# A hybrid encoder block on one core: the opening of its projection, the order of its tokens and the shape of its last products rearranged

## The chip, the cores and the metric

One core of a Trainium2 chip runs the kernel. The metric is the device time of one execution in microseconds (us), median over runs. The engines are TensorE (PE; its weight loads are shown apart as PEld), VectorE (DVE), ScalarE (ACT), GpSimd (POOL) and SyncE (SP), which here only starts DMAs.

## The reference

One layer over 256 tokens of width 1024, all in float32:

```python
h = rmsnorm(x, norm_gain)
z = h @ w_in                       # 8192 columns: pool-in, pool-gate, q, k, v, attention gate, merge gates
a_in, a_gate, q, k, v, b_gp, g_logits = split(z)
y_a = (multiscale_pool(a_in, w_pool, pool_scale) * silu(a_gate)) @ w_proj_a
att = dilated_attention(q, k, v, rel_bias)     # 3 groups of 8 heads, (window, dilation) (128,1) (512,4) (2048,16)
y_b = (att * silu(b_gp)) @ w_proj_b
gates = sigmoid(g_logits + b_gate)
merged = gates[0] * y_a + gates[1] * y_b
return rmsnorm(x + merged @ w_out, final_gain)
```

## The kernel before

**Split products.** A float32 product is made of three passes: each operand is cut into a high part (a copy rounded to fp32r) and a low part (the operand minus its high part), and `mm3` (L253) multiplies high by high, high by low and low by high into one PSUM accumulator. The normalised tokens are `hh` and `hl`, 128 x 8 x 256 each, with the 1024 channels on partitions in eight blocks `kc`, and the 256 tokens sorted by their residue modulo 4.

**Weights.** SP streams all weights in the order of the list `order` (L82 to L90) through four buffers `wraw`: 31 tiles of `w_in` with 256 columns each (1 MB), then the pooling map, the two branch projections and `w_out`. `cut_half` (L116) makes half a tile's high part on ACT (L128) and its low part on DVE (L133), and starts the next load when a buffer is free. The cuts run two tiles ahead of the products.

**The opening (L170 to L250).** Its order on ACT, DVE, PE and POOL is written out by hand. PE first multiplies a zero tile (`keep_warm`, L177): 12 calls, two instructions each. The two blocks of 128 tokens come by DMA; their mean squares are taken on ACT and DVE, POOL makes the reciprocal root (L191), and DVE and ACT scale half the columns each (`XN`, L194 and L195). DVE copies the two halves (four `kc` rows each) of weight tile 0 to its high part (L197), and behind each copy POOL makes that half's low part (`cut_lo`, L163). PE turns `XN` over with 8 transposes a block (`turn`, L202), two `keep_warm` calls behind the first block and one behind the second. Per `kc`, ACT then writes `hh` (L228) and DVE `hl` (L229) out of PSUM, read with a step of four tokens so that they land by residue. PE takes tile 0 (`part0`, L207): per `kc` a pair of high by high products and a pair of high by low ones, two `kc` behind ACT and DVE; the pairs with the low weights follow for `kc` 0 to 3 behind step 5 and for 4 to 7 at the end, and then three small products for the bias lines (L245). Then `cut_next` makes both parts of tiles 1 and 2. The fills of the bias table (L486) are tied behind POOL's last low part.

**The middle.** Key, query, value, pooling, gate and attention stages follow, all as products with the 256 tokens; the rest of the order is the scheduler's.

**The end (L638 to L731).** `out_mm(kh, nh, tb)` (L674) multiplies token block `tb` with columns `nh` (512) and channels `kh` (half of them): 12 products of 512 columns, but for `nh` = `tb` = 1, which goes as two times 256. Behind the second half of the channels DVE adds the residual `XL` (L689), ACT squares with a sum (L691), DVE multiplies by the gain (L695), `finish` (L701) adds the sums on DVE and takes the root on POOL (L710), and `store` (L713) scales columns 0 to 639 on DVE and the rest on ACT and sends the block in two DMAs of 64 tokens, one by SP and one by ACT, with DRAM rows 4 apart. `XL` is loaded by POOL in four DMAs of 64 tokens (L661).

Of the kernel before, what the change touches and what calls it, by code (L numbers as in the profile page):

```python
# [11 lines left out]
F32 = mybir.dt.float32  # L12
# [17 lines left out]
LROW = 9  # L30
LAG_T, LAG_O = 2, 2
RATES = 0.5, 0.667
WARM = 12, 2, 1
CUT = 640
POOL_W = (2, 4, 8, 16)
PAD = 8
# [6 lines left out]
def encoder_block(ctx: ExitStack, tc: tile.TileContext, x, w_in, lines, w_pool, w_proj_a, w_proj_b,  # L43
# [126 lines left out]
    with tc.manual_schedule(engines={mybir.EngineType.Activation, mybir.EngineType.DVE, mybir.EngineType.PE,  # L170
                                    mybir.EngineType.Pool}):
        tiny = sb.tile([P, 1], F32, name="tiny")
        warm = sb.tile([P, P], F32, name="warm")
        nc.vector.memset(warm, 0.0)
        nc.scalar.activation(tiny, warm[:, 0:1], AF.Square)

        def keep_warm(times):  # L177
            for _ in range(times):
                nc.tensor.matmul(misc[:, P:2 * P], warm, warm, start=True, stop=True)

        keep_warm(WARM[0])
        halves = [slice(h * 512, (h + 1) * 512) for h in range(2)]
        for b in range(2):
            sq = [slot([P, 512], F32, "st", f"sq{b}{h}", 3) for h in range(2)]
            nc.scalar.activation(sq[0], X[:, b, halves[0]], AF.Square, scale=1.0 / 32.0, accum_out=ss[:, b, 0:1])
            xb = X[:, b, halves[1]]
            nc.vector.tensor_tensor_reduce(sq[1], xb, xb, scale=1.0 / D, scalar=EPS, op0=ALU.mult, op1=ALU.add,
                                           accum_out=ss[:, b, 1:2])
            t = slot([P, 1], F32, "rt", f"rt{b}", 2)
            nc.vector.tensor_tensor(t, ss[:, b, 0:1], ss[:, b, 1:2], op=ALU.add)  # L190
            nc.gpsimd.tensor_tensor(rs[:, b:b + 1], t, mhalf, op=ALU.pow)  # L191
        open_parts(0)
        for b in range(2):
            nc.vector.tensor_scalar(XN[:, b, halves[0]], X[:, b, halves[0]], rs[:, b:b + 1], None, op0=ALU.mult)  # L194
            nc.scalar.activation(XN[:, b, halves[1]], X[:, b, halves[1]], AF.Copy, scale=rs[:, b:b + 1])  # L195
        for k in (0, 4):
            nc.vector.tensor_copy(parts[0][0][:, k:k + 4, :], raws[0][0][:, k:k + 4, :])  # L197
            first_lo = cut_lo(0, k, k + 4, nc.gpsimd)
        tps = [bank([P, 2, S], "mm" if i < 3 else "T", f"tp{i}", 3 if i < 3 else 2) for i in range(4)]

        def turn(kc, b):
            nc.tensor.transpose(tps[kc % 4][:, kc // 4, b * P:(b + 1) * P], XN[:, b, kc * P:(kc + 1) * P], ident)  # L202

        acc = bank([P, 2, 512], "S", "k00", 1)
        acc0 = [acc[:, u, 0:S] for u in range(2)]

        def part0(kc, lo):  # L207
            hi_, lo_ = parts[0]
            for u in range(2):
                c = slice(u * P, (u + 1) * P)  # L210
                if not lo:
                    nc.tensor.matmul(acc0[u], hi_[:, kc, c], hh[:, kc, :], start=kc == 0, stop=False)
                else:
                    nc.tensor.matmul(acc0[u], lo_[:, kc, c], hh[:, kc, :], start=False, stop=kc == KC - 1)
            for u in range(0 if lo else 2):
                c = slice(u * P, (u + 1) * P)
                nc.tensor.matmul(acc0[u], hi_[:, kc, c], hl[:, kc, :], start=False, stop=False)

        for kc in range(KC):
            turn(kc, 0)  # L220
        keep_warm(WARM[1])
        for kc in range(KC):
            turn(kc // 2 + kc % 2 * 4, 1)
        keep_warm(WARM[2])
        for kc in range(KC):
            v = tps[kc % 4][:, kc // 4].rearrange("p (j r) -> p r j", r=4)
            gcol = prm[:, kc:kc + 1]
            nc.scalar.activation(hh[:, kc, :].rearrange("p (r j) -> p r j", r=4), v, AF.Copy, scale=gcol)  # L228
            nc.vector.scalar_tensor_tensor(hl[:, kc, :].rearrange("p (r j) -> p r j", r=4), v, gcol,  # L229
                                           hh[:, kc, :].bitcast(F32).rearrange("p (r j) -> p r j", r=4),  # L230
                                           op0=ALU.mult, op1=ALU.subtract)
            if kc >= 2:
                part0(kc - 2, False)
            if kc == 5:
                for k in range(4):
                    part0(k, True)
        part0(6, False)
        part0(7, False)
        for kc in range(4, 8):
            part0(kc, True)  # L240

        for t in range(3):
            w = 3 * NH
            o = 3 * P + t // 2 * w
            nc.tensor.matmul(misc[:, t * w:(t + 1) * w], oh[:, t * P:(t + 1) * P], oh[:, o:o + w],  # L245
                             start=True, stop=True)
        cut_next()
        nc.vector.tensor_copy(line.rearrange("p i r h -> p r i h"),
                              misc[:, 0:LROW * NH].rearrange("p (r i h) -> p r i h", i=2, h=4))
        cut_next()  # L250
# [404 lines left out]
        nc.vector.tensor_tensor(ML[:, cb, :], GA[:, cb, :], MH[:, cb, :].bitcast(F32), op=ALU.subtract)  # L655

    XL = slot([P, 2, D], F32, "v", "XL", 2)
    xr = x2.rearrange("(j r) d -> r j d", r=4)
    orr = o2.rearrange("(j r) d -> r j d", r=4)
    for r in range(4):  # L660
        nc.gpsimd.dma_start(XL[(r % 2) * 64:(r % 2) * 64 + 64, r // 2, :], xr[r])  # L661
    fg = slot([P, D], F32, "uu", "fg")
    nc.gpsimd.dma_start(fg, final_gain.rearrange("(o d) -> o d", o=1).to_broadcast([P, D]))

# [3 lines left out]
    accs = {}  # L668
    both = bank([P, 2, 512], "S", "both", 1)
    wo = {}  # L670
    so = sb.tile([P, 2, 3], F32, name="so")
    Y = slot([P, 2, D], F32, "q", "Y")

    def out_mm(kh, nh, tb):  # L674
        hi, lo = wo[kh, nh]
        c = slice(tb * P, (tb + 1) * P)
        cuts = 2 if (nh, tb) == (1, 1) else 1
        w = 512 // cuts
        for i in range(cuts):
            if kh == 0:  # L680
                accs[nh, tb, i] = both[:, tb, :] if nh == 0 else bank([P, w], "mm", f"out{nh}{tb}{i}", 3)
            acc = accs[nh, tb, i]
            for k in range(4):
                kc = kh * 4 + k
                mm3(acc, MH[:, kc, c], ML[:, kc, c], hi[:, k, i * w:(i + 1) * w], lo[:, k, i * w:(i + 1) * w],
                    kc == 0, kc == KC - 1)
            if kh == 1:
                cols = slice(nh * 512 + i * w, nh * 512 + (i + 1) * w)
                nc.vector.tensor_tensor(XL[:, tb, cols], acc, XL[:, tb, cols], op=ALU.add)  # L689
                j = slot([P, 512], F32, "st", f"j{tb}{nh}{i}", 3)  # L690
                nc.scalar.activation(j[:, :w], XL[:, tb, cols], AF.Square, scale=1.0 / 32.0,  # L691
                                     accum_out=so[:, tb, nh + i:nh + i + 1])
                if (nh, i) == (1, cuts - 1):
                    finish(tb, cuts)
                nc.vector.tensor_tensor(Y[:, tb, cols], XL[:, tb, cols], fg[:, cols], op=ALU.mult)  # L695
        if (kh, nh) == (1, 1):
            store(tb)

    scales = {}

    def finish(tb, cuts):  # L701
        t = slot([P, 1], F32, "nm", f"s2{tb}", 3)
        if cuts == 2:
            t0 = slot([P, 1], F32, "rl", f"s1{tb}", 3)
            nc.vector.tensor_tensor(t0, so[:, tb, 0:1], so[:, tb, 1:2], op=ALU.add)
            nc.vector.tensor_scalar(t, t0, so[:, tb, 2:3], EPS, op0=ALU.add, op1=ALU.add)
        else:
            nc.vector.tensor_scalar(t, so[:, tb, 0:1], so[:, tb, 1:2], EPS, op0=ALU.add, op1=ALU.add)
        r2 = slot([P, 1], F32, "l", f"r2{tb}", 3)
        nc.gpsimd.tensor_tensor(r2, t, mhalf, op=ALU.pow)  # L710
        scales[tb] = r2

    def store(tb):  # L713
        r2 = scales[tb]
        nc.vector.tensor_scalar(Y[:, tb, 0:CUT], Y[:, tb, 0:CUT], r2, None, op0=ALU.mult)
        nc.scalar.activation(Y[:, tb, CUT:], Y[:, tb, CUT:], AF.Copy, scale=r2)
        for rl in range(2):
            (nc.sync, nc.scalar)[rl].dma_start(orr[2 * tb + rl], Y[rl * 64:rl * 64 + 64, tb, :])

    wo[0, 0] = weights(n)  # L720
    for tb in range(2):
# [50 lines left out]
def _layout(x, norm_gain, w_in, b_gate, rel_bias, w_pool, pool_scale, w_proj_a, w_proj_b, w_out, final_gain):  # L772
# [11 lines left out]
    for k in range(3):  # L784
        for j, g in enumerate((0, k)):
# [4 lines left out]
    prm.append(np.broadcast_to(edges.reshape(1, -1), (P, edges.size)))  # L790
    prm.append(np.zeros((P, NPRM - sum(a.shape[1] for a in prm)), np.float32))
    w_out = np.concatenate([cols(w, 512) for w in np.split(np.asarray(w_out)[0], 2)])
    out = {"x": x, "w_in": cols(np.asarray(w_in)[0], 256), "lines": lines.reshape(99, -1),
           "w_pool": np.asarray(w_pool)[0].transpose(1, 0, 2), "w_proj_a": cols(np.asarray(w_proj_a)[0], 512),
           "w_proj_b": cols(np.asarray(w_proj_b)[0], 512), "w_out": w_out, "final_gain": final_gain,
# [24 lines left out]
```

## Time and profile before

| | us |
|---|---|
| median of three runs (lowest, highest) | 263.88 (263.72, 265.59) |
| the profiled execution: its own time | 264.12 |
| its span, first to last instruction | 262.30 |
| PE busy | 249.7 |
| DVE busy | 209.3 |
| ACT busy | 164.6 |
| POOL busy | 72.6 |

The span is what the trace covers; the profiled execution's own time holds 1.82 us around it. Times in the trace count from the span's start. Merged rows give a start, the time from the first start to the last end, and a count.

### The profile page before, as it was taken

The numbers are of one execution on the slowest core, as the hardware profiler recorded it, in microseconds if no ns is written. First come the engines' busy times: TensorE is split into PE (matmuls) and PEld (weight loads), VectorE is DVE, ScalarE is ACT, GpSimd is POOL, SyncE is SP. The second block draws the span as 40 slices with busy tenths as digits, with TensorE's granted clock in tenths as the row PEclk, the third lists the DMA queues.
The fourth block names the chain that finished last, engine by engine and source line by source line (L and its number), as shares of the span: only waits on it lengthen the run. The fifth ranks groups of instructions, "written<-read, shape, count | busy, mean of one in ns | idle before, by whom it ended". The sixth has DMA issues, their size and how long they took to land.

```text
span 262.3 us, 5321 instructions
## 1 busy us (share of the span) xinstructions
PE 249.7 (95%) x2088; PEld 245.0 (93%) x2088; DVE 209.3 (80%) x397; ACT 164.6 (63%) x283; POOL 72.6 (28%) x103
## 2 busy tenths in 40 slices
PE   7599999999999999999999999999999999999980
PEld 6599999999999999999999999999999999988870
DVE  2889989768888787889697997967859988899271
ACT  4597755666656566658976778665557798445140
POOL 1643391000799200010673920000010040442000
PEclk9999999999999999999999999999999999999996
DMA  6998999985444744444889967154440699300033
GB/s 230 388 413 314 224 331 288 344 316 184 161 162 160 239 164 162 161 160 152 256 250 227 313 216 295 41 162 160 162 160 0 214 325 282 146 4 0 0 80 80
DMA packets 9479, 51.99 MB, mean 198 GB/s; under 512 B 1147, under 2 KB 1374, under 8 KB 4206
## 3 DMA queue, kind: packets, MB, share of 16 engines
q1 hardware_dynamic: 6606, 43.95, 48.0%
q0 software_dynamic: 2544, 7.12, 12.6%
q10 hardware_dynamic: 304, 0.59, 0.6%
q8 instruction: 16, 0.26, 0.4%
q14 instruction: 9, 0.07, 0.1%
HBM read 47.42 MB, written 1.09 MB: 185 GB/s over the span
## 4 chain that ended last, share of the span: by engine, by line
PE 81%; DVE 6%; issue 4%; ACT 3%; DMA 3%; SPq 0%; POOLq 0%; POOL 0%; ACTq 0%
PE q L254 4%; PE v L254 4%; PE v L256 4%; PE v L255 4%; PE q L255 4%; PE q L256 4%; PE g L254 4%; PE g L256 4%; PE g L255 4%; PE k L254 4%; PE k L255 3%; PE k L256 3%; DMA wraw<-in_w_in_dram 3%; PE y L254 2%; PE y L256 2%
## 5 line engine op out<-in xcount | busy, mean ns | idle before, releaser
L133 DVE TENSOR_TENSOR wlo<-wraw,whi 128x512 fp32r<-128x512 f32 (+2 forms) x134 | 107.8, 844 | 8.4 <-ACT whi L128 7.5
L128 ACT ACTIVATE whi<-wraw 128x1024 fp32r<-128x1024 f32 (+1 forms) x80 | 80.8, 1038 | 23.1 <-PE q L255 8.6
L254 PE MATMUL g<-hh,whi 128*128 128x256 f32 x128 | 35.8, 280 | 0.0
L256 PE MATMUL g<-hh,wlo 128*128 128x256 f32 x128 | 35.4, 276 | 0.0
L255 PE MATMUL g<-hl,whi 128*128 128x256 f32 x128 | 35.3, 276 | 0.0
L311 ACT ACTIVATE st<-st,nm 128x512 f32<-128x512 f32 x16 | 11.6, 723 | 29.7 <-DVE nm L308 29.7
L254 PE MATMUL q<-hh,whi 128*128 128x256 f32 x96 | 26.6, 277 | 0.1
L254 PE MATMUL v<-whi,hh 128*128 128x256 f32 x96 | 26.6, 277 | 0.0
L256 PE MATMUL v<-whi,hl 128*128 128x256 f32 x96 | 26.5, 276 | 0.0
L255 PE MATMUL v<-wlo,hh 128*128 128x256 f32 x96 | 26.5, 276 | 0.0
L255 PE MATMUL q<-hl,whi 128*128 128x256 f32 x96 | 26.5, 276 | 0.0
L256 PE MATMUL q<-hh,wlo 128*128 128x256 f32 x96 | 26.5, 276 | 0.0
L254 PEld LDWEIGHTS g<-hh,whi 128*128 128x128 f32 x128 | 24.0, 188 | 0.1
L255 PEld LDWEIGHTS g<-hl,whi 128*128 128x128 f32 x128 | 24.0, 188 | 0.0
L256 PEld LDWEIGHTS g<-hh,wlo 128*128 128x128 f32 x128 | 24.0, 188 | 0.0
L254 PE MATMUL k<-hh,whi 128*128 128x256 f32 x80 | 22.3, 278 | 0.0
L256 PE MATMUL k<-hh,wlo 128*128 128x256 f32 x80 | 22.1, 277 | 0.0
L255 PE MATMUL k<-hl,whi 128*128 128x256 f32 x80 | 22.1, 277 | 0.0
L254 PEld LDWEIGHTS q<-hh,whi 128*128 128x128 f32 x96 | 18.0, 188 | 0.3 <-issue 0.3
L255 PEld LDWEIGHTS v<-wlo,hh 128*128 128x128 f32 x96 | 18.0, 188 | 0.0
L256 PEld LDWEIGHTS v<-whi,hl 128*128 128x128 f32 x96 | 18.0, 188 | 0.0
L254 PEld LDWEIGHTS v<-whi,hh 128*128 128x128 f32 x96 | 18.0, 188 | 0.0
(176 smaller groups left out, 732.4 us busy)
## 6 DMA issues: line engine op xcount, KB each, us to landing
wraw<-in_w_in_dram SPq DMA_DIRECT2D x31, 1024.0 KB, 5.5
wraw<-in_w_out_dram SPq DMA_DIRECT2D x4, 1024.0 KB, 6.4
T<-line_d POOLq DMA_DIRECT2D x4, 576.0 KB, 6.3
KX<-KX POOLq DMA_DIRECT2D x8, 256.0 KB, 12.9
wraw<-in_w_proj_a_dram SPq DMA_DIRECT2D x2, 1024.0 KB, 4.7
wraw<-in_w_proj_b_dram SPq DMA_DIRECT2D x2, 1024.0 KB, 4.9
X<-in_x_dram SPq DMA_DIRECT2D x2, 512.0 KB, 4.2
wraw<-in_w_in_dram SPq DMA_DIRECT2D x2, 512.0 KB, 6.7
```

Source lines behind the costliest of these rows:

```text
L128: nc.scalar.activation(hi[:, s, :], t[:, s, :], AF.Copy)
L133: nc.vector.tensor_tensor(lo[:, s, :], t[:, s, :], hi[:, s, :].bitcast(F32), op=ALU.subtract)
L254: nc.tensor.matmul(acc, ah, bh, start=first, stop=False)
L255: nc.tensor.matmul(acc, ah, bl, start=False, stop=False)
L256: nc.tensor.matmul(acc, al, bh, start=False, stop=last)
L311: e = nc.scalar.activation(st, st, AF.Exp, bias=nm, scale=-1.0, accum_out=l)
```

## The change

- **Opening.** All 15 `keep_warm` calls stand at the start, none between the transposes. DVE makes both copies of tile 0 first; then POOL makes the low part in two instructions, of five `kc` rows and of three. `part0` takes one pass at a time: high by high for `kc` right behind ACT and DVE, high by low two steps later, and all low-weight pairs at the end, with the three bias-line products between `kc` 4 and 5.
- **Tokens.** The host sorts `x` by residue and sorts the result back; `hh` and `hl` are read out of PSUM without a step, `XL` comes in two DMAs of 128 rows.
- **End.** All `out_mm` products have 256 columns, each 256-column quarter with a PSUM bank of its own. The sums of squares run along in one value per block (`run`); for the last quarter DVE makes the sum itself, from the running one, in place of ACT and of DVE's adds. `store` sends columns 0 to 319 and 320 to 639 by SP, each behind its own DVE scaling, and 640 to 1023 by ACT, all 128 rows each.

```diff
-WARM = 12, 2, 1
+WARM = 15
...
         for k in (0, 4):
             nc.vector.tensor_copy(parts[0][0][:, k:k + 4, :], raws[0][0][:, k:k + 4, :])
-            first_lo = cut_lo(0, k, k + 4, nc.gpsimd)
+
+        cut_lo(0, 0, 5, nc.gpsimd)
+        first_lo = cut_lo(0, 5, 8, nc.gpsimd)
...
-        def part0(kc, lo):
+        def part0(kc, x):
             hi_, lo_ = parts[0]
             for u in range(2):
                 c = slice(u * P, (u + 1) * P)
...
+                nc.tensor.matmul(acc0[u], (lo_ if x == 2 else hi_)[:, kc, c], (hl if x == 1 else hh)[:, kc, :],
+                                 start=x == 0 and kc == 0, stop=x == 2 and kc == KC - 1)
...
-        keep_warm(WARM[1])
         for kc in range(KC):
             turn(kc // 2 + kc % 2 * 4, 1)
-        keep_warm(WARM[2])
         for kc in range(KC):
-            v = tps[kc % 4][:, kc // 4].rearrange("p (j r) -> p r j", r=4)
+            v = tps[kc % 4][:, kc // 4]
             gcol = prm[:, kc:kc + 1]
...
+            nc.scalar.activation(hh[:, kc, :], v, AF.Copy, scale=gcol)
+            nc.vector.scalar_tensor_tensor(hl[:, kc, :], v, gcol, hh[:, kc, :].bitcast(F32), op0=ALU.mult,
+                                           op1=ALU.subtract)
+            part0(kc, 0)
             if kc >= 2:
-                part0(kc - 2, False)
+                part0(kc - 2, 1)
+        for kc in (6, 7):
+            part0(kc, 1)
+        for kc in range(KC):
             if kc == 5:
...
+                for t in range(3):
+                    w = 3 * NH
+                    o = 3 * P + t // 2 * w
+                    nc.tensor.matmul(misc[:, t * w:(t + 1) * w], oh[:, t * P:(t + 1) * P], oh[:, o:o + w],
+                                     start=True, stop=True)
+            part0(kc, 2)
...
-    for r in range(4):
-        nc.gpsimd.dma_start(XL[(r % 2) * 64:(r % 2) * 64 + 64, r // 2, :], xr[r])
+    for tb in range(2):
+        nc.gpsimd.dma_start(XL[:, tb, :], x2[tb * P:(tb + 1) * P, :])
...
+    def quarter(nh, tb, i):
+        if nh == 0:
+            return both[:, i, 0:S] if tb == 0 else bank([P, S], "T", f"out{nh}{tb}{i}", 2)
+        o = (tb, i) == (0, 0)
+        return bank([P, S], "O" if o else "mm", f"out{nh}{tb}{i}", 1 if o else 3)
...
+        for i in range(2):
             if kh == 0:
...
+                accs[nh, tb, i] = quarter(nh, tb, i)
             acc = accs[nh, tb, i]
+            cs = slice(i * S, (i + 1) * S)
             for k in range(4):
                 kc = kh * 4 + k
...
+                mm3(acc, MH[:, kc, c], ML[:, kc, c], hi[:, k, cs], lo[:, k, cs], kc == 0, kc == KC - 1)
...
+            q = 2 * nh + i
+            cols = slice(q * S, (q + 1) * S)
+            nc.vector.tensor_tensor(XL[:, tb, cols], acc, XL[:, tb, cols], op=ALU.add)
+            j = slot([P, S], F32, "st", f"j{tb}{q}", 3)
+            part = so[:, tb, q:q + 1]
+            if q == 3:
+
+                nc.vector.tensor_tensor_reduce(j, XL[:, tb, cols], XL[:, tb, cols], scale=1.0 / D, scalar=run[tb],
+                                               op0=ALU.mult, op1=ALU.add, accum_out=part)
+                finish(tb, part)
+            else:
+                nc.scalar.activation(j, XL[:, tb, cols], AF.Square, scale=1.0 / 32.0, accum_out=part)
+                t = slot([P, 1], F32, "nm", f"s{tb}{q}", 3)
+                nc.vector.tensor_scalar(t, part, run.get(tb, EPS), None, op0=ALU.add)
+                run[tb] = t
+            nc.vector.tensor_tensor(Y[:, tb, cols], XL[:, tb, cols], fg[:, cols], op=ALU.mult)
...
     def store(tb):
         r2 = scales[tb]
-        nc.vector.tensor_scalar(Y[:, tb, 0:CUT], Y[:, tb, 0:CUT], r2, None, op0=ALU.mult)
+        rows = slice(tb * P, (tb + 1) * P)
+        for cols in (slice(0, CUT // 2), slice(CUT // 2, CUT)):
+            nc.vector.tensor_scalar(Y[:, tb, cols], Y[:, tb, cols], r2, None, op0=ALU.mult)
+            nc.sync.dma_start(o2[rows, cols], Y[:, tb, cols])
         nc.scalar.activation(Y[:, tb, CUT:], Y[:, tb, CUT:], AF.Copy, scale=r2)
-        for rl in range(2):
-            (nc.sync, nc.scalar)[rl].dma_start(orr[2 * tb + rl], Y[rl * 64:rl * 64 + 64, tb, :])
+        nc.scalar.dma_start(o2[rows, CUT:], Y[:, tb, CUT:])
...
+    x = np.asarray(x).reshape(1, S // 4, 4, D).transpose(0, 2, 1, 3).reshape(1, S, D)
...
+    return np.ascontiguousarray(r.results[0]["out_0_dram"].reshape(1, 4, S // 4, D).transpose(0, 2, 1, 3)
+                                ).reshape(1, S, D)
```

## Rows read from the trace of the kernel before

**Rows 1.** Busy time by engine, sum of eight stretches that cover 18.00 to 254.80.
```profile
sum 236.80, PE 236.35 PEld 232.04 DVE 196.42 ACT 151.88 POOL 64.19; mean PE 29.54 PEld 29.00 DVE 24.55 ACT 18.99 POOL 8.02
```

**Rows 2.** Chain of work that ended last, opening: start, us, what.
```profile
9.25 2.38 issue
```

**Rows 3.** Timeline, DVE, opening: start, us, what, count, idle before and its releaser.
```profile
8.04 0.69 DVE L197 CAST whi<-wraw 128x1024 fp32r<-128x1024 f32 x1
9.21 2.49 DVE L197 CAST whi<-wraw 128x1024 fp32r<-128x1024 f32 x1 [0.49 <-DMA wraw<-in_w_in_dram]
11.63 3.21 DVE L229 SCALAR_TENSOR_TENSOR hl<-tp,prm,hh 128x256 fp32r<-128x256 f32 x8
14.77 2.36 DVE L133 TENSOR_TENSOR wlo<-wraw,whi 128x1024 fp32r<-128x1024 f32 x2
```

**Rows 4.** Timeline, POOL, opening.
```profile
8.80 2.35 POOL L163 TENSOR_TENSOR wlo<-wraw,whi 128x1024 fp32r<-128x1024 f32 x1 [1.20 <-DVE whi L197]
11.78 2.40 POOL L163 TENSOR_TENSOR wlo<-wraw,whi 128x1024 fp32r<-128x1024 f32 x1 [0.63 <-DVE whi L197]
```

**Rows 5.** Timeline, PE, opening.
```profile
1.05 4.59 PE L179 MATMUL misc<-warm 128*128 128x128 f32 x24 [1.05 <-DVE warm L174]
...
13.85 1.07 PE L214 MATMUL k<-hh,wlo 128*128 128x256 f32 x8
...
17.48 0.75 PE L245 MATMUL misc<-oh 99*128 99x24 f32 x6
18.07 0.36 PE L254 MATMUL k<-hh,whi 128*128 128x256 f32 x1
```

**Rows 6.** Timeline, PE, DVE, ACT and POOL, behind the last product.
```profile
254.49 0.28 PE L256 MATMUL out<-whi,ML 128*128 128x256 f32 x1
...
254.81 0.42 DVE L689 TENSOR_TENSOR XL<-out,XL 128x256 f32<-128x256 f32 x1 [0.19 <-PE out L256]
...
255.26 0.42 ACT L691 ACTIVATE j<-XL 128x256 f32<-128x256 f32 x1 [0.84 <-DVE XL L689]
...
256.10 0.55 POOL L710 TENSOR_TENSOR r<-s,mhalf 128x1 f32<-128x1 f32 x1 [4.47 <-DVE s L706]
...
256.69 0.55 DVE L715 TENSOR_SCALAR Y<-Y,r 128x640 f32<-128x640 f32 x1 [0.67 <-POOL r L710]
...
257.33 0.50 ACTq L718 DMA_DIRECT2D out_dram<-Y  x1
```

**Rows 7.** Timeline, ACT, opening.
```profile
9.04 1.57 ACT L228 ACTIVATE hh<-tp,prm 128x256 fp32r<-128x256 f32 x4 [0.68 <-PE tp L202]
...
13.68 3.89 ACT L128 ACTIVATE whi<-wraw 128x1024 fp32r<-128x1024 f32 x4
```

**Rows 8.** Timeline, DVE and POOL, around 36 us.
```profile
35.70 3.48 DVE L133 TENSOR_TENSOR wlo<-wraw,whi 128x1024 fp32r<-128x1024 f32 x1 [1.16 <-ACT whi L128]
...
33.52 3.40 POOL L479 COPY BT<-T 128x384 f32<-128x384 f32 x4
36.88 3.40 POOL L484 COPY BT<-T 64x256 f32<-64x256 f32 x4
```

**Rows 9.** Timeline, PE, out projection: the first product of each group.
```profile
240.76 0.28 PE L254 MATMUL out<-whi,MH 128*128 128x256 f32 x1
...
243.49 0.39 PE L254 MATMUL both<-whi,MH 128*128 128x512 f32 x1
...
246.28 0.39 PE L254 MATMUL out<-whi,MH 128*128 128x512 f32 x1
```

**Rows 10.** DMA issues: queue, count, KB each, median us to landing.
```profile
out_dram<-Y SPq DMA_DIRECT2D x2, 256.0 KB, 3.0
out_dram<-Y ACTq DMA_DIRECT2D x2, 256.0 KB, 3.7
wraw<-in_w_pool_dram SPq DMA_DIRECT2D x1, 256.0 KB, 2.6
```

**Rows 11.** Busy time, 10 to 12 us: stretch, length, PE, PEld, DVE, ACT, POOL, clock, DMA.
```profile
10.00:12.00 2.00, 0.12 (x2) 0.00 (x0) 2.00 (x2) 0.61 (x2) 1.37 (x2) 1.00 1.03 360
```

More of the change, by code (lines that the diff above doesn't have):

```diff
@@ L179, in keep_warm @@
                 nc.tensor.matmul(misc[:, P:2 * P], warm, warm, start=True, stop=True)
-        keep_warm(WARM[0])
+        keep_warm(WARM)
         halves = [slice(h * 512, (h + 1) * 512) for h in range(2)]
@@ L210, in part0 @@
                 c = slice(u * P, (u + 1) * P)
[L211 to L217, printed above, removed]
+                nc.tensor.matmul(acc0[u], (lo_ if x == 2 else hi_)[:, kc, c], (hl if x == 1 else hh)[:, kc, :],
+                                 start=x == 0 and kc == 0, stop=x == 2 and kc == KC - 1)
@@ L219, in encoder_block @@
         for kc in range(KC):
             turn(kc, 0)
-        keep_warm(WARM[1])
         for kc in range(KC):
             turn(kc // 2 + kc % 2 * 4, 1)
-        keep_warm(WARM[2])
         for kc in range(KC):
-            v = tps[kc % 4][:, kc // 4].rearrange("p (j r) -> p r j", r=4)
+            v = tps[kc % 4][:, kc // 4]
             gcol = prm[:, kc:kc + 1]
[L228 to L231, printed above, removed]
+            nc.scalar.activation(hh[:, kc, :], v, AF.Copy, scale=gcol)
@@ L232, in encoder_block @@
+            nc.vector.scalar_tensor_tensor(hl[:, kc, :], v, gcol, hh[:, kc, :].bitcast(F32), op0=ALU.mult,
+                                           op1=ALU.subtract)
+            part0(kc, 0)
             if kc >= 2:
-                part0(kc - 2, False)
+                part0(kc - 2, 1)
+        for kc in (6, 7):
+            part0(kc, 1)
+        for kc in range(KC):
             if kc == 5:
[L235 to L246, printed above, removed]
+                for t in range(3):
[3 more added lines that the diff above has]
+                                     start=True, stop=True)
@@ L657, in encoder_block @@
     XL = slot([P, 2, D], F32, "v", "XL", 2)
-    xr = x2.rearrange("(j r) d -> r j d", r=4)
-    orr = o2.rearrange("(j r) d -> r j d", r=4)
-    for r in range(4):
-        nc.gpsimd.dma_start(XL[(r % 2) * 64:(r % 2) * 64 + 64, r // 2, :], xr[r])
+    for tb in range(2):
+        nc.gpsimd.dma_start(XL[:, tb, :], x2[tb * P:(tb + 1) * P, :])
     fg = slot([P, D], F32, "uu", "fg")
@@ L670, in encoder_block @@
     wo = {}
-    so = sb.tile([P, 2, 3], F32, name="so")
+    so = sb.tile([P, 2, 4], F32, name="so")
     Y = slot([P, 2, D], F32, "q", "Y")
+    def quarter(nh, tb, i):
[3 more added lines that the diff above has]
+        return bank([P, S], "O" if o else "mm", f"out{nh}{tb}{i}", 1 if o else 3)
     def out_mm(kh, nh, tb):
@@ L676, in out_mm @@
         c = slice(tb * P, (tb + 1) * P)
-        cuts = 2 if (nh, tb) == (1, 1) else 1
-        w = 512 // cuts
-        for i in range(cuts):
+        for i in range(2):
             if kh == 0:
-                accs[nh, tb, i] = both[:, tb, :] if nh == 0 else bank([P, w], "mm", f"out{nh}{tb}{i}", 3)
+                accs[nh, tb, i] = quarter(nh, tb, i)
             acc = accs[nh, tb, i]
+            cs = slice(i * S, (i + 1) * S)
             for k in range(4):
                 kc = kh * 4 + k
[L685 to L695, printed above, removed]
@@ new lines, in out_mm @@
+                mm3(acc, MH[:, kc, c], ML[:, kc, c], hi[:, k, cs], lo[:, k, cs], kc == 0, kc == KC - 1)
+            if kh == 0:
+                continue
+            q = 2 * nh + i
[12 more added lines that the diff above has]
+                run[tb] = t
@@ L696, in out_mm @@
+            nc.vector.tensor_tensor(Y[:, tb, cols], XL[:, tb, cols], fg[:, cols], op=ALU.mult)
         if (kh, nh) == (1, 1):
             store(tb)
[L699 to L708, printed above, removed]
+    run, scales = {}, {}
@@ L709, in finish @@
+    def finish(tb, t):
         r2 = slot([P, 1], F32, "l", f"r2{tb}", 3)
@@ L818 @@
     r = _run(nc, [arrays], core_ids=[0])
-    return r.results[0]["out_0_dram"]
+    return np.ascontiguousarray(r.results[0]["out_0_dram"].reshape(1, 4, S // 4, D).transpose(0, 2, 1, 3)
+                                ).reshape(1, S, D)
```

## The prediction

> **What bounds the kernel now.** I read the busy times by stretch first, then the chain of waits, then the timelines of the two places that the chain leaves PE. From 18.00 to 254.80 PE is busy for 236.35 of 236.80 us [rows 1]: the stream of products has no hole, and no other engine sets its length. What is left is the opening (PE starts tile 1 at 18.07 [rows 5]) and the end: the last product begins at 254.49 and lasts 0.28, so it ends at T = 254.77 [rows 6], 7.53 us before the span does at 262.30. So the span is 18.07 + 236.70 + 7.53.
>
> In the opening, the chain has 2.38 us that it can put on nothing [rows 2]. The timelines show what they are: DVE's second copy of tile 0 takes 2.49 us where the first takes 0.69 [rows 3]. POOL's first low part runs from 8.80 to 11.15 [rows 4]; the copy ends at 11.70, 0.55 behind it. DVE's copy stands until POOL's instruction is over. Everything behind the copy on DVE, all eight `hl`, is late by that.
>
> **The opening, step by step.** POOL now starts behind both copies. The second starts at 9.21, when its load lands, and with 0.69 is done at 9.90 [rows 3]. The eight `hl` took 3.21 us beside a POOL low part that was no slower (2.40 against 2.35) [rows 3, 4], so I let both run at full pace: one `hl` per 0.40, the first done at 10.4, the last at 13.13. POOL came 0.08 behind the copy (11.70 to 11.78) [rows 3, 4], so it starts at 9.98; five `kc` rows are 5/4 of 2.35 = 2.94, to 12.92, and three are 1.76, to 14.68.
>
> PE: eight products take 1.07 us with 0.28 for the last one, so one starts every (1.07 - 0.28)/7 = 0.113 us and a pair is 0.227 [rows 5]. The high by high pairs of `kc` 0 to 2 go before 10.4; ACT's `hh` come from 9.04 at four in 1.57 us [rows 7], and are not late. At 10.4 there are 13 pairs left that need no low weights: 2.95 us, to 13.4; the pair behind the last `hl` (13.13 + 0.23) gives the same. Then five low pairs, 1.14, to 14.5; POOL has had their rows since 12.92. The bias-line products take 18.07 - 17.48 = 0.59 [rows 5], to 15.1, and cover the wait for the other three rows (14.68). Three pairs, 0.68: tile 1 starts at 15.8, not 18.07. **Opening: -2.27.** Of other prices here: the 15 warm calls are six instructions more in front; 24 took 4.59 us from 1.05 [rows 5], so 30 end by 6.8 at the latest, before the transposes, which wait for `XN`; those taken out lay between transposes that ACT and DVE pace. Reading PSUM without a step I count at nothing, since PE then waits for no `hl`. If it is faster, PE still needs its 13 pairs.
>
> What is late next is tile 1's low part. ACT is done with `hh` at about 12.2, and its copies take 3.89/4 = 0.97 [rows 7], so half of tile 1 is ready for DVE at 13.2, when POOL's second part is running. Around 36 us a low part on DVE takes 3.48 us beside POOL's copies [rows 8], where two take 2.36 elsewhere [rows 3]. So I let DVE wait: 14.68 + 1.18 = 15.86. The third product of tile 1, at 15.8 + 0.23 = 16.03, is the first that needs it: free, with 0.17 to spare. The second half (17.04) is needed four `kc` (4 x 0.34) later, at 17.4. SP's load of tile 4 waits for POOL's last low part, 14.68 in place of 14.18 [rows 4]; three tiles of 48 x 0.113 = 5.4 us lie before its products. What POOL does behind it (the fills, the line store, the bias table) is first used tens of us later, when the scores begin.
>
> **The end.** Twelve products of 512 columns take 246.28 - 243.49 = 2.79 us, 24 of 256 take 243.49 - 240.76 = 2.73 [rows 9]: 0.0050 per former 512. There are 96 - 24 = 72 of those: **-0.36**. The new banks come from stages long over. `XL` in two DMAs takes two issues off POOL, which is far ahead there: nothing.
>
> Behind T, the add, ACT's square and DVE's small add lead to POOL's root at 256.10 = T + 1.33 [rows 6]. Now DVE squares and sums itself behind the add (T + 0.46). No row shows this at 256 columns; ACT's square takes 0.42 and the add 0.42, so I take 0.53 with its readout and let it lie between 0.42 and 0.83 (no gain). The root starts at T + 1.03, 0.30 sooner, and ACT's store goes at T + 2.26, not 257.33 = T + 2.56 [rows 6]. SP's first goes at about T + 2.0, behind a scaling between half and all of 0.55 (I take 0.38); its second at T + 2.6, behind the first one's issue (0.50, as ACT's). The stores of before land 3.0 and 3.7 us behind their issue [rows 10], the last at T + 6.26. The last one now, 160 KB, lies between 2.6 (a load of 256 KB that had the queues nearly to itself) and 3.7: T + 5.2 to T + 6.3. I take 3.1, nearest to SP's own: T + 5.7, **-0.5**, the 0.30 contained in it.
>
> Against that, DVE's load: a quarter costs an add and a product (0.42 each) and a small add, about 1.0; the last quarter of block 0 costs 0.42 + 0.53 + 0.42 and two scalings, 2.1. Between the two blocks' last products (48 x 0.114 = 5.46 us) that is 5.1 us of work, and in it lie waits for the root (0.55) and for ACT's squares, which stand behind ACT's own scaling. Block 1's last add is then late by between 0 and 0.7. I take **+0.2**.
>
> Sum: -2.27 - 0.36 - 0.5 + 0.2 = -2.9. Against the profiled execution 264.12 becomes 261.2; that one lies 0.24 above the median of 263.88, for which I say **261.0**.
>
> **Rivals.**
> *POOL loses its turn.* If DVE gets tile 1's low part in between POOL's two instructions, POOL's three rows come at 12.92 + 1.18 + 1.76 = 15.86, and with 0.68 tile 1 starts at 16.54: 261.7; if both halves go first, 17.04 + 0.68 = 17.7 and 262.9. For it: DVE is ready at 13.2, only 0.3 after POOL's second starts, and ACT may be faster. Against it: DVE's instruction of 35.70 ended at 39.18, so it ran from about 38.0, and POOL's row of copies went on at 36.88 with DVE standing [rows 8]: POOL back to back kept its turn. The Trainium skill (SBUF — State Buffer, Who interferes with whom) says that whichever of two such instructions is issued first has the shared port for its whole length. By that, DVE would go first if its instruction were issued before 12.92, with the 261.7 of above; the row at 35.70 speaks against a plain order of issue. Chance 0.17.
>
> *The end gives more.* Stores that land in 2.6 us and no crowding on DVE: -2.27 - 0.36 - 1.06 = -3.7, 260.2. For it: the first third of the bytes goes half a us sooner. Against: the same bytes have to go, in shorter rows. Chance 0.15.
>
> *The end gives nothing.* DVE is 0.7 late and the stores take 3.7: -2.27 - 0.36 + 0.7 = -1.9, 262.0. For it: 5.1 us of work in 5.46. Chance 0.1.
>
> *Slower: the clock.* With no warm products among the transposes, PE could be put to 1.2 GHz at about 10 us. Each us at the low level loses half a us of products, so it decides from 5.9 us at the low level; 8 us would cost 4.0, and with the gain of 2.9 make 265.0. Against it: from 10 to 12 us PE was busy for 0.12 of 2.00 us and kept a granted clock of 1.00 [rows 11], and the changed opening has no hole that long. Chance 0.04.
>
> **How the numbers follow.** The forecast has 0.54, with 260.3 to 261.7 of its own from the bounds of stores and DVE. A measurement of this kernel can tell about 1%, 2.64 us: faster means below 261.24. That holds seven in ten of the forecast (0.38) and the better end (0.15), with the rivals of 261.7 and above in between: 0.52, 0.43 and, with the clock, 0.05 for slower. The range goes from 259.8 to 262.9; the clock and the far ends of the others lie outside.
>
> **What would show it.** Both copies of tile 0 at 0.69; the first `hl` at 9.9; POOL's two parts near 2.9 and 1.8 and done by 14.7; tile 1's first product at 15.8; DVE's first low part of tile 1 stretched to 2.5 or so, ending near 15.9; products of 256 columns 0.114 apart to the end; the root 1.0 behind the last product, and the span's end 7.2 behind it. I am wrong if the second copy still stands behind POOL, if PE's pairs are over 0.23 apart before 16, if the low pairs wait for POOL, if the stream between opening and end is longer or shorter than 236.3 by more than half a us, or if DVE's last add is far behind the last product.

## The result, and the profile after

The changed kernel takes 260.89 us (median, 260.81 to 261.02), the kernel before 263.81 beside it: ratio 0.9852, 95% interval 0.9811 to 0.9893. Executions of the kernel before lie in two groups, 263.7 to 264.6 and 265.5 to 266.5 us; ratios and intervals here are taken over both, and against the median of the lower group alone the changed kernel is at 0.989. 261.0 had been forecast, in a range from 259.8 to 262.9.

The span went from 262.30 to 259.0, by 3.3 us. That is the forecast's 2.9 and a little more, but not by its terms. Cut at the same four places, the two profiles give:

| us | before | after | difference | forecast |
|---|---|---|---|---|
| start to tile 1 | 18.07 | 15.83 | -2.24 | -2.27 |
| tile 1 to first branch projection | 191.86 | 191.50 | -0.36 | 0 |
| branch projections | 22.43 | 22.94 | +0.51 | 0 |
| out projection to T | 22.41 | 22.64 | +0.23 | -0.36 |
| T to the span's end | 7.53 | 6.09 | -1.44 | -0.3 |

The opening came as worked out. The timeline of the changed kernel, DVE then POOL then PE, against [rows 3 to 5]:

```profile
9.10 0.69 DVE L197 CAST whi<-wraw 128x1024 fp32r<-128x1024 f32 x1 [0.41 <-DMA wraw<-in_w_in_dram]
9.71 3.22 DVE L224 SCALAR_TENSOR_TENSOR hl<-tp,prm,hh 128x256 fp32r<-128x256 f32 x8
12.87 4.00 DVE L133 TENSOR_TENSOR wlo<-wraw,whi 128x1024 fp32r<-128x1024 f32 x2
...
9.87 4.79 POOL L163 TENSOR_TENSOR wlo<-wraw,whi 128x1280 fp32r<-128x1280 f32 x2 [2.30 <-DVE whi L197]
...
12.79 1.87 POOL L163 TENSOR_TENSOR wlo<-wraw,whi 128x768 fp32r<-128x768 f32 x1
...
14.48 0.75 PE L237 MATMUL misc<-oh 99*128 99x24 f32 x6
...
15.83 0.28 PE L247 MATMUL k<-hh,whi 128*128 128x256 f32 x1
```

The second copy takes 0.69 and no longer 2.49; the eight `hl` keep their 3.22 and start 1.92 sooner. POOL's two parts (the second, of three rows, is shown alone again below them) end at 14.66 (forecast 14.68), before PE asks for the last rows. DVE's first two low parts of tile 1 take 4.00 together where [rows 3] has 2.36: the first stood behind POOL's second part, and PE did not wait for it. In the six other profiles with this opening tile 1 starts between 15.83 and 16.04.

The end, same view (PE, DVE, POOL, ACT and SP), against [rows 6]; then the DMA issues, against [rows 10]:

```profile
252.63 0.28 PE L249 MATMUL out<-whi,ML 128*128 128x256 f32 x1
...
252.95 0.42 DVE L687 TENSOR_TENSOR XL<-out,XL 128x256 f32<-128x256 f32 x1
253.41 0.48 DVE L692 CUSTOM_DVE_ANT_0 j<-XL,s 128x256 f32<-128x256 f32 x1
...
253.98 0.67 POOL L708 TENSOR_TENSOR r<-so,mhalf 128x1 f32<-128x1 f32 x1 [4.75 <-DVE so L692]
...
255.33 0.34 ACTq L718 DMA_DIRECT2D out_dram<-Y  x1
...
255.10 0.81 SPq L716 DMA_DIRECT2D out_dram<-Y  x2
```

```profile
out_dram<-Y SPq DMA_DIRECT2D x4, 160.0 KB, 2.4
out_dram<-Y ACTq DMA_DIRECT2D x2, 192.0 KB, 2.1
```

T is 252.91. DVE's last add starts 0.04 behind it: no crowding. The root starts at T + 1.07 (forecast 1.03), but takes 0.67 and not 0.55, with DVE's last product beside it. What was far off is the landing: 2.1 to 2.4 us and not 3.1.

### The profile page after: what moved, and what is told of

Its sections match the earlier page's. It is cut to its first block, busy times and chain, and to the rows that moved or that the text cites. A ratio compares the mean times of both kernels' runs of the same rounds, so it can differ in the third digit from the quotient of the medians.

```text
span 259.0 us, 5482 instructions
## 1 busy us (share of the span) xinstructions
PE 250.4 (97%) x2160; PEld 248.8 (96%) x2160; DVE 210.2 (81%) x412; ACT 164.4 (63%) x285; POOL 74.5 (29%) x101
## 4 chain that ended last, share of the span: by engine, by line
PE 84%; DVE 6%; issue 3%; ACT 2%; DMA 2%; POOLq 0%; POOL 0%; SPq 0%; DVEq 0%; ACTq 0%
PE v L249 4%; PE v L248 4%; PE q L249 4%; PE q L248 4%; PE v L247 4%; PE q L247 4%; PE g L247 4%; PE g L248 4%; PE g L249 4%; PE k L247 4%; PE k L249 4%; PE k L248 4%; PE y L247 2%; PE y L248 2%; PE y L249 2%
## 5 line engine op out<-in xcount | busy, mean ns | idle before, releaser
L249 PEld LDWEIGHTS q<-hh,wlo 128*128 128x128 f32 x96 | 18.0, 188 | 0.0
L248 PEld LDWEIGHTS q<-hl,whi 128*128 128x128 f32 x96 | 18.0, 188 | 0.0
```

The lines of the kernel that those rows point to most:

```text
L248: nc.tensor.matmul(acc, ah, bl, start=False, stop=False)
L249: nc.tensor.matmul(acc, al, bh, start=False, stop=last)
```

## The experiments

**The changed kernel again.** No edit.

> The changed kernel once more, to see whether the pace of its products is a property of the program or of one execution. In the first profile PE's products of 256 columns start every 0.1134 us in most stretches and every 0.1178 us in others: 267 of them in a row from 212.0 to 243.5 us, where the kernel before ran at 0.1136 behind the same stall. Theory A (the program's own timing decides): the same stretches are slow again, 260.9 us. Theory B (chance of one execution): the stretch behind 212 us is fast in this one, and the span is about 267 x 0.0044 = 1.2 us shorter, 259.7 us.

Measured: 260.59 us, ratio 0.9856 (0.9837 to 0.9876). The branch projections took 22.40 us, as before the change, and not 22.94; the out projection 22.97. So the slow pace behind 212 us was that one execution's (theory B there), but the 1.2 us were not won: the out projection was slow in both, here to its end. In the branch projections the pace moves from execution to execution, so the +0.51 of the table is not the change's. The out projection is steadier: in all nine profiles with quarters its first 96 products and more run at 0.1176 to 0.1178 us.

**The opening alone**, in the kernel before.

```diff
-WARM = 12, 2, 1
+WARM = 15
...
-            first_lo = cut_lo(0, k, k + 4, nc.gpsimd)
+        cut_lo(0, 0, 5, nc.gpsimd)
+        first_lo = cut_lo(0, 5, 8, nc.gpsimd)
...
+            part0(kc, 0)
             if kc >= 2:
-                part0(kc - 2, False)
+                part0(kc - 2, 1)
```

> Kernel before with the opening alone changed (both copies first, POOL's low parts of five and three rows behind them, one pass at a time, all warm products in front); tokens, XL, products and stores as before. Theory A (the opening is worth what the two profiles show, 18.07 against 15.83, and nothing behind it takes it back): 263.8 - 2.24 = 261.6 us, with the end's 7.5 us as before. With the stall of 0.4 us at 40 us gone too: 261.2. Rival (the change's gain is mostly the end's, and the stream gives the opening back): 262.5 us or more.

Measured: 261.87 us, ratio 0.9907 (0.9886 to 0.9928); by the medians 2.3 us are gained. Tile 1 starts at 16.12, with the tokens still read by a step; the end takes 7.57 us from T, as before. Theory A: this is the larger half of the gain, and it needs none of the rest.

**The end and the sorted tokens alone**, with the opening of before.

```diff
-WARM = 15
+WARM = 12, 2, 1
...
-        cut_lo(0, 0, 5, nc.gpsimd)
-        first_lo = cut_lo(0, 5, 8, nc.gpsimd)
+            first_lo = cut_lo(0, k, k + 4, nc.gpsimd)
...
```

> Changed kernel with the opening of before (POOL behind each copy, passes mixed, warm products between the transposes); sorted tokens, quarters and stores by columns stay. Theory A (the end is worth 7.53 - 6.09 = 1.4 us by the two profiles, the products of 256 columns gain up to 0.36): between 262.0 and 262.6 us. If the slow pace of products behind 212 us belongs to the end's new order, 0.5 to 1.2 of that is taken back: 262.6 to 263.5 us. Rival (stores gain nothing alone): 263.8 us.

Measured: ratio 0.9968 (0.9946 to 0.9991), 263.23 us, but with executions from 262.49 to 264.70. The stretch from T is 6.14 us, so the stores gain alone too. The seven executions below 264 have their median at 262.82, above theory A's 262.0 to 262.6 and within the sum for a slow pace; the profile has that pace in its branch projections (22.93 us). The profiled execution is one of 264.67, and its stages show why (columns: stretch, length, PE, PEld, DVE, ACT, POOL, then granted clock, DMA share, GB/s):

```profile
10.00:12.00 2.00, 0.12 (x2) 0.00 (x0) 2.00 (x2) 0.61 (x2) 1.37 (x2) 1.00 1.06 356
12.00:13.00 1.00, 0.83 (x5) 0.84 (x6) 1.00 (x4) 0.85 (x3) 1.00 (x1) 0.74 0.96 385
13.00:14.00 1.00, 1.00 (x6) 1.00 (x6) 1.00 (x4) 1.00 (x4) 1.00 (x1) 0.50 0.96 401
14.00:15.00 1.00, 1.00 (x7) 1.00 (x6) 1.00 (x4) 1.00 (x2) 0.96 (x5) 0.50 1.01 418
15.00:16.00 1.00, 1.00 (x7) 1.00 (x6) 1.00 (x2) 1.00 (x2) 0.26 (x2) 0.55 1.02 426
```

Behind the hole from 10 to 12 us the granted clock falls to 0.50, the lower level of 1.2 GHz, until about 16; PE does 6 or 7 products a us in place of 12. Tile 1 starts at 19.71. Only this execution of the slower five was profiled.

**The hole filled**, in that kernel.

```diff
-WARM = 12, 2, 1
+WARM = 12, 2, 9
```

> The changed kernel with the opening of before (the run that ended at 262.5 to 263.3 us in some executions and at 264.2 to 264.7 in others, and whose profile shows a granted clock of 0.50 from 12.5 to 15.6 us), now with nine warm products in place of one behind the transposes, so that PE is busy in the hole from 10 to 12 us; nothing else waits for them. Theory A (the hole lets the clock fall in part of the executions, and that is the 1.6 us between the two groups): all executions in the lower group, 262.5 to 263.0 us, granted clock 1.00 from 12 to 16 us. Rival (the two groups have another cause): again executions above 264 us.

Measured: 262.54 us; of twelve executions ten lie within 262.46 to 262.59, one at 263.46 (the profiled one) and one at 264.76, against five of twelve above 264 without the products. The same stages:

```profile
10.00:12.00 2.00, 1.91 (x17) 1.70 (x16) 2.00 (x2) 0.62 (x2) 1.37 (x2) 1.00 1.04 364
12.00:13.00 1.00, 0.84 (x7) 0.84 (x8) 1.00 (x4) 0.86 (x3) 1.00 (x1) 1.00 0.97 393
13.00:14.00 1.00, 1.00 (x12) 1.00 (x11) 1.00 (x4) 1.00 (x4) 1.00 (x1) 1.00 1.03 426
```

Tile 1 starts at 18.09, 1.62 sooner. The profile fits theory A, but one execution of twelve still went above 264, as the rival had it, and five of twelve against one of twelve can be chance: that the hole causes the fall is likely, and not shown. The profiled 263.46 has another reason, its middle part (tile 1 to the first branch projection): 192.39 us, with the stand shown next and the slow pace from 42 to 63 us. The changed opening has no hole, and none of its eight timed executions lies above 261.02.

This profile also explains the -0.36 of the table's second line. Its low part of 35.73 meets POOL's bias copies as in [rows 8], and PE stands behind it. DVE, POOL, PE, and then PE in the kernel before:

```profile
35.73 3.47 DVE L133 TENSOR_TENSOR wlo<-wraw,whi 128x1024 fp32r<-128x1024 f32 x1 [1.17 <-ACT whi L128]
...
33.55 3.39 POOL L478 COPY BT<-T 128x384 f32<-128x384 f32 x4
...
39.83 0.28 PE L255 MATMUL q<-hh,wlo 128*128 128x256 f32 x1
40.22 0.35 PE L253 MATMUL q<-hh,whi 128*128 128x256 f32 x1
```

```profile
39.80 0.28 PE L256 MATMUL q<-hh,wlo 128*128 128x256 f32 x1
40.20 0.36 PE L254 MATMUL q<-hh,whi 128*128 128x256 f32 x1
40.40 0.28 PE L255 MATMUL q<-hl,whi 128*128 128x256 f32 x1
```

Elsewhere a product starts every 0.113 us; here the next two come after 0.40 and 0.20, together 0.37 late. Only these two of the thirteen profiles have the stand, and their middle parts are the longest, 191.86 and 192.39 us; in the others it takes 191.37 to 191.50. In the changed kernel the copies wait for their table's DMA and start as DVE does; the two take turns, and DVE's longest low part there is 1.78:

```profile
33.15 5.36 POOL L472 COPY BT<-T 128x384 f32<-128x384 f32 x4 [1.30 <-DMA T<-line_d]
...
33.33 1.78 DVE L133 TENSOR_TENSOR wlo<-wraw,whi 128x1024 fp32r<-128x1024 f32 x1 [0.48 <-ACT whi L128]
```

But that start is not needed for it. The run with the end alone, whose stream is 1.6 us later here, has the low part as far into the same copies as the kernel before (2.17 us behind their start, there 2.18), and DVE goes next, behind the copy that was running. DVE, POOL:

```profile
37.34 1.49 DVE L133 TENSOR_TENSOR wlo<-wraw,whi 128x1024 fp32r<-128x1024 f32 x1 [1.17 <-ACT whi L128]
...
35.17 4.41 POOL L478 COPY BT<-T 128x384 f32<-128x384 f32 x4
```

That the stand is gone is therefore not shown to be the changed opening's doing.

**POOL between the copies again**, in the changed kernel.

```diff
-        cut_lo(0, 0, 5, nc.gpsimd)
-        first_lo = cut_lo(0, 5, 8, nc.gpsimd)
+            first_lo = cut_lo(0, k, k + 4, nc.gpsimd)
```

> Changed kernel, with POOL's low part right behind each of VectorE's two copies again (four and four rows); one pass at a time stays. Theory A (the second copy stands behind POOL's first instruction, and all hl are late by that): the second copy takes about 2.5 us, the first hl starts at 11.6 and not 9.7, tile 1 starts near 17.6 to 17.8, +1.8 to +2.0 us: 262.7 to 262.9 us. Rival (the order of the passes is what gained): the copy is late but tile 1 still starts before 16.5 us, 261.5 us or less.

Measured: 262.69 us, ratio 0.9934 (0.9914 to 0.9954), 2.1 above the changed kernel beside it. DVE:

```profile
9.24 2.46 DVE L197 CAST whi<-wraw 128x1024 fp32r<-128x1024 f32 x1 [0.54 <-DMA wraw<-in_w_in_dram]
11.62 3.21 DVE L222 SCALAR_TENSOR_TENSOR hl<-tp,prm,hh 128x256 fp32r<-128x256 f32 x8
```

Theory A: the second copy and the first `hl` are back where they were in [rows 3]. (The profiled execution, 263.72, has the low clock behind PE's hole as well, and tile 1 at 19.35; the others lie between 262.24 and 262.75 and were not profiled, so tile 1's forecast start at the full clock was not seen.)

**Four low pairs early again**, in the changed kernel.

```diff
+            if kc == 5:
+                for k in range(4):
+                    part0(k, 2)
...
-        for kc in range(KC):
+        for kc in range(4, KC):
```

> Changed kernel with the low-weight pairs of kc 0 to 3 behind step 5 again, as before, and the others at the end. POOL's first five rows are done near 12.8 us; PE reaches the place at about 12.0. Theory A (putting all low pairs last is what hides POOL's later start): PE stands up to 0.8 us there, tile 1 starts near 16.4 in place of 15.9, +0.3 to +0.8 us against the changed kernel. Rival (the order of the passes is worth nothing, POOL behind the copies is all): within 0.2 us.

Measured: 261.55 us, ratio 0.9890 (0.9852 to 0.9928). PE:

```profile
12.95 1.20 PE L213 MATMUL k<-hh,wlo 128*128 128x256 f32 x8 [0.74 <-POOL wlo L163]
...
16.93 0.28 PE L250 MATMUL k<-hh,whi 128*128 128x256 f32 x1
```

PE stands 0.74 us for POOL and tile 1 starts 0.9 to 1.1 later than in the profiles with the changed opening (15.83 to 16.04), more than expected; the changed kernel was not run beside this one. Theory A: it is the low pairs at the end that make POOL's later start free.

**Stores of 64 rows again**, in the changed kernel.

```diff
-        for cols in (slice(0, CUT // 2), slice(CUT // 2, CUT)):
-            nc.vector.tensor_scalar(Y[:, tb, cols], Y[:, tb, cols], r2, None, op0=ALU.mult)
-            nc.sync.dma_start(o2[rows, cols], Y[:, tb, cols])
+        nc.vector.tensor_scalar(Y[:, tb, 0:CUT], Y[:, tb, 0:CUT], r2, None, op0=ALU.mult)
...
-        nc.scalar.dma_start(o2[rows, CUT:], Y[:, tb, CUT:])
+        for rl in range(2):
+            o = tb * P + rl * 64
+            (nc.sync, nc.scalar)[rl].dma_start(o2[o:o + 64, :], Y[rl * 64:rl * 64 + 64, tb, :])
```

> Changed kernel with the stores of before: per block one scaling of 640 columns on VectorE, then two DMAs of 64 tokens with all columns, one by SP and one by ACT (rows now contiguous in DRAM). Theory A (the shape of the stores is the end's main gain: landing 2.1 to 2.4 us for 128 rows against 3.0 to 3.7 for 64 rows): landings return to 3.0 to 3.7 us, the time from the last product to the span's end from 6.1 to about 7.2 us, +1.1 us on the changed kernel's ratio of 0.986, so about 0.990. Rival (the earlier start of the first store and the shorter way to the root are the gain): +0.3 us, 0.987.

Measured: 261.48 us, ratio 0.9881 (0.9833 to 0.9928). T to the end is 7.44 us, and the landings are those of before:

```profile
out_dram<-Y SPq DMA_DIRECT2D x2, 256.0 KB, 3.0
out_dram<-Y ACTq DMA_DIRECT2D x2, 256.0 KB, 3.7
```

The ratio lies between the two that were expected and does not decide; the stretch from T and the landings do, for theory A. The DRAM rows are contiguous here and were 4 apart before, with the same landings, so that is not it. The shorter way to the root, still in this kernel, is worth 0.1 of the 1.44.

**Two stores of 128 rows**, in the changed kernel.

```diff
-        for cols in (slice(0, CUT // 2), slice(CUT // 2, CUT)):
-            nc.vector.tensor_scalar(Y[:, tb, cols], Y[:, tb, cols], r2, None, op0=ALU.mult)
-            nc.sync.dma_start(o2[rows, cols], Y[:, tb, cols])
+        nc.vector.tensor_scalar(Y[:, tb, 0:CUT], Y[:, tb, 0:CUT], r2, None, op0=ALU.mult)
+        nc.sync.dma_start(o2[rows, 0:CUT], Y[:, tb, 0:CUT])
```

> Changed kernel with two stores a block in place of three, each of 128 rows: columns 0 to 639 by SP behind one scaling, 640 to 1023 by ACT. Theory A (128 rows are what counts, the third store little): within 0.3 us of the changed kernel, landing below 2.8 us. Rival (starting the first third of the bytes early is what counts): +0.5 us or more.

Measured: 260.55 us, ratio 0.9845 (0.9804 to 0.9885); T to the end 6.33, against 6.09 to 6.18 with three. Theory A: the shape of the stores counts (7.44 against 6.33), the early third is worth 0.2. Nor is it the bytes of one store: SP's is larger here and lands sooner.

```profile
out_dram<-Y SPq DMA_DIRECT2D x2, 320.0 KB, 2.5
out_dram<-Y ACTq DMA_DIRECT2D x2, 192.0 KB, 2.6
```

What the runs do not part: stores of 64 rows also have the longer rows, 4 KB each. The packets in the trace show one thing more. With 64 rows ACT's first packet starts 1.3 us behind SP's first, when SP's are almost done; with 128 rows it starts 0.5 us behind it, and the two stores run side by side.

**512 columns a product**, in the changed kernel.

```diff
...
-        for i in range(2):
+        cuts = 2 if (nh, tb) == (1, 1) else 1
+        w = 512 // cuts
+        for i in range(cuts):
...
```

> Changed kernel whose out projection takes 512 columns a product again (as before, but for the last group); what follows the products stays in quarters. Theory A of the prediction (two of 256 columns take 0.2276 us, one of 512 takes 0.2325): +0.36 us. Rival, from the pace of the first profiles (0.1178 us a product in most of the end's stretch, so 0.2356 a pair): no gain was there to lose, and the out projection is 0 to 0.2 us shorter with 512 columns. In the profile: from the first product of the out projection to the end of the last one 22.4 us (as before) against 22.6 (as changed).

Measured: 260.37 us, ratio 0.9833 (0.9794 to 0.9873); the out projection takes 22.60 us, with quarters 22.64 and 22.97. The rival: nothing had been gained. The one group of 24 products with 256 columns ran at 0.1135 us in the kernel before, where the forecast took its pace (240.76 to 243.49 in [rows 9]); in all three later profiles with 512 columns it runs at 0.1178, here from 238.15 to 240.98.

**A fourth bank for the branch projections**, in the changed kernel, and the same with 512 columns.

```diff
-                acc = mmb(f"y{n}{u}")
+                acc = mmb(f"y{n}{u}") if u < 3 else bank([P, S], "T", f"y{n}{u}", 2)
```

> Changed kernel with a fourth PSUM bank for the branch projections (every fourth accumulator in one of the two banks that the attention left). In the profiles PE stands twice there for a bank that VectorE has not read yet (0.41 us at 211.4 and 0.1 to 0.2 at 228.3), and behind the second stand the products run at 0.1176 to 0.1178 us in place of 0.1134, for 123 products or more. Theory A (the slow pace begins with such a stand and stays until the next one): both stands go, the products run at 0.1134 to the end, 0.55 + 0.5 = about 1.0 us less, 259.5 us on the scale of 260.5 to 260.9. Theory B (the slow pace belongs to what the products read or write in this stretch): the stands go, the pace stays, -0.5 us.

> The same fourth bank, with 512 columns a product in the out projection. If the pace behind the stands decides what 256 columns are worth: at 0.1134 a product 256 columns win 72 x 0.005 = 0.36 us (this run 0.3 to 0.4 us above the one with quarters). If both run at the slow pace again, they are level, or 512 columns are ahead by up to 0.2 us.

Measured: 259.91 us, ratio 0.9831 (0.9804 to 0.9858), and 259.72, ratio 0.9821 (0.9795 to 0.9848). Both stands are gone, and the branch projections take 21.83 and 21.84 us. But the pace changes all the same, with the first product of the out projection and no stand before it (PE, the version with 256 columns; first its branch projection, then its out projection; twelve products from the one row to the other, then 48):

```profile
226.77 0.28 PE L249 MATMUL y<-ATHL,wlo 128*128 128x256 f32 x1
...
228.13 0.28 PE L249 MATMUL y<-ATHL,wlo 128*128 128x256 f32 x1
```

```profile
229.26 0.28 PE L247 MATMUL both<-whi,MH 128*128 128x256 f32 x1
...
234.91 0.28 PE L247 MATMUL out<-whi,MH 128*128 128x256 f32 x1
```

The first gives 1.36/12 = 0.1133 a product, the second 5.65/48 = 0.1177. So neither theory holds as it stood: the stands are worth 0.5 us of their own, and a slow pace can begin without one. With 512 columns the out projection takes 22.60, with 256 22.64. These two are the fastest versions run; their intervals overlap that of the changed kernel, which was not run beside them; not one execution of the first lies above 260.50 or, of the second, above 260.04, and the changed kernel's eight lie from 260.25 to 261.02.

## Why the prediction was right, and where its terms were not

- **The opening** was right in every step: the copy free of POOL, `hl` at full pace beside it, POOL's parts, the 13 pairs, the low pairs covered by the bias-line products. The runs that put back POOL's place (+2.1 by the medians) and the early low pairs (tile 1 0.9 to 1.1 later) show both halves needed.
- **POOL loses its turn** did not happen. DVE stood behind POOL's second part, as the 3.48 of [rows 8] had it; it was ready at 12.87, 0.08 behind the start of that part (12.79). The Trainium skill (SBUF — State Buffer, Who interferes with whom) has the two exclude each other by order of issue: here POOL was first by that too, so the opening does not tell that order from a kept turn. Around 36 us neither holds in every run: in [rows 8] DVE stood from 35.70 to about 38.0 while POOL began further copies, so the two did not go in the order in which their rows start; in the run with the end alone DVE was let in from the same place behind one copy (the 1.49 at 37.34), so POOL did not keep its turn. So the argument against this rival was one execution's, and what decides stays open.
- **"The new banks", "0.0050 per former 512", -0.36**: wrong. I took the pace of 256 columns from one stretch of one execution (0.1138 between 240.76 and 243.49) for all of it. In most of the out projection it is 0.1175, where two of 256 (0.235) are no shorter than one of 512 (0.2325 to 0.2333). The run with 512 columns shows nothing lost.
- **The stores, -0.5**: the mechanism was taken wrongly. I counted the earlier first third and took the landing (3.1) from stores of 64 rows; the shape of the stores decides. Of the 1.44 us, 1.1 go with the shape (7.44 against 6.33 from T to the end), 0.2 with the early third and 0.1 with the way to the root.
- **Crowding on DVE, +0.2**: none. The last add starts 0.04 behind T.
- **What the earlier stream meets** I counted at nothing; it is -0.36: the collision of [rows 8] cost PE nearly 0.4 us at 39.80. The rows that I used for DVE's waiting stood there; I did not follow them to PE. Whether the two collide is not settled by the opening, as the run with the end alone shows.
- **The clock** I feared in the changed opening. It fell in both profiles of runs that had POOL between the copies again and the hole unfilled, and in none with the changed opening. The row that I held against it, a clock of 1.00 across the hole [rows 11], was one execution's; of the kernel before, no execution of the upper group was profiled.
- **My own signs of being wrong**: one came true. The stream between opening and end was to be 236.3 us within half a us; it took 237.08 (236.76 in the repeat, just inside). Of what would show the forecast, the products were not 0.114 apart to the end, and the span ended 6.1 and not 7.2 behind T.

So the opening was right by its mechanism, and the rest was luck: two terms of the end were off by +0.6 and -1.1, two unforeseen ones by -0.36 and +0.5, and together they come to -0.4.

## What to carry to other kernels

Where two engines keep each other from the same instructions, let the one whose result is needed first go through and put the consumers of the other last; both moves were needed. Here a store of all 128 rows, cut by columns, ended sooner than two of 64 rows; try that shape before cutting a store by rows. A pace or a clock that one profile shows is one execution's: look at a second one before a term of a few tenths is taken from it.

## What the runs showed that I had not expected

- A store of 64 rows with 4 KB each lands 3.0 to 3.7 us behind its issue, one of 128 rows with 1.25 to 2.5 KB each in 2.1 to 2.6 (medians), with the same bytes in all.
- Products of the same shape have two paces, 0.1134 and 0.1176 to 0.1178 us, at a granted clock of 1.00 in both. In the attention stage and the projections the pace stays over tens of products and changes at a stand or where other products come in between, but not at each and not in every execution the same. What sets it stays open.
- Behind a hole of 2 us in PE's work the granted clock fell to 0.50 in the profiled execution of one program, at 1.6 us, and stayed at 1.00 in that of another with the same hole.
- A DVE low part that became ready during the third of POOL's bias copies stood through three more in one profile (3.48 us) and was let in behind the third in another (1.49 us), at the same distance from the start of the copies.
- POOL's root takes 0.67 to 0.69 us with DVE's product of two SBUF tiles beside it and 0.55 to 0.57 without, in every profile.
